# Bias broadcasts of the first layer issued from GpSimd behind marker copies, and two more weight-chunk buffers from the first layer on

## The chip, the core and the metric

The kernel runs on one core of one Trainium2 chip. The time is device microseconds (us) of that core. In the text PE is TensorE, DVE is VectorE, ACT is ScalarE, POOL is GpSimd and SP is SyncE. Each of these engines works through its own list of instructions in order. A transfer (DMA) is started by an instruction in the list of SP, ACT or POOL, and all transfers then run on the same 16 DMA engines.

## What is computed

The program is a whole small network on 512 tokens of width 1024: a first block of two layers and a second block with a state-space mixer and a convolutional feed-forward. The change touches only the first layer of the first block and a table that later attention stages use:

```python
def short_conv_mixer(h, w_in, conv_w, w_out):
    b_gate, c_gate, u = jnp.split(h @ w_in, 3, axis=-1)
    v = c_gate * u
    vp = jnp.pad(v, ((0, 0), (CONV_WIDTH - 1, 0), (0, 0)))
    conv = sum(conv_w[k] * vp[:, k:k + S] for k in range(CONV_WIDTH))
    return (b_gate * conv) @ w_out

def squared_relu_mlp(h, w1, w2):
    return jnp.square(jax.nn.relu(h @ w1)) @ w2
...
        bias_w = jnp.transpose(bias_g[t5_bucket(d_w)], (0, 2, 3, 1))   # d_w: query position minus key position
        logit_w = jnp.einsum('bqghd,bkgd->bqghk', qt, kw) + bias_w[None]
```

The attention bias depends only on the distance of query and key, so for each head it is one line of numbers, shifted by one element from one query to the next.

## The kernel before, in words

**Weights.** All weight matrices lie in DRAM as 362 chunks of 128x1024 f32 (512 KB), in the order in which PE will take them. `Stream.pre` (L188) loads a chunk ahead into a buffer `w32` (two buffers) with a DMA issued by SP (L195), and splits it by halves of 128x512 into a high part `whi` (ACT, L214) and a low part `wlo` (DVE, L216), four buffers each. Three matmuls of 128x128 by 128x512 (high by high, high by low, low by high) use each 128x128 block, so a chunk is 8 x 3 = 24 matmuls. PE takes `whi` and `wlo`; the buffers of a half come free when PE has finished with the half four before it, and a `w32` buffer comes free when both its halves are split. While the field `ap` of the stream is set, that is in the two MLP stages (chunks 34 to 95 and 135 to 196), two chunks of every four go into two further buffers `ax`, so that four chunks are held.

**First layer.** `layer_a` (L516) makes eight blocks f = 0 to 7 of the gated convolution. A block is three products of 24 matmuls each (c, u and b gate, one chunk apiece), then a short run on DVE and ACT: `cc`, `v`, three convolution steps `cv`, `b`, the block's output `o` (L561), and its split `yh` (ACT, L320) and `yl` (DVE, L321). Five tiles per block come from a ring of ten. The products lie in seven PSUM buffers. Then eight products with `a_w_out` follow, and the MLP.

**Bias lines.** In block f = 1 `biases` (L609) computes the 16 lines of numbers with six small matmuls and stores them to DRAM as `line` (SP, L625; the scheduler puts its parts between other work, so that it ends in block 3). `skew_out` (L635) then broadcasts a stretch of a head's line to 128 rows of a DRAM table `sk`, each row one element longer than the stretch, so that a later plain read sees every row shifted by one. There are 48 such DRAM-to-DRAM transfers: 16 of 128x640 (320 KB), 16 of 128x384 (192 KB) and 16 of 128x144 (72 KB). `skew_out` is called after each product from block 2 on, two transfers a call, and they are issued by ACT (L638). The tables are first read at 629 us, in the attention stage.

**Order.** A scheduler orders each engine's list when the program is built. `keep_in_program_order` keeps the transfers in the order of the code among themselves. Each DMA signals its landing on one of eight semaphores that are handed out in turn, and a DMA that gets a semaphore still in use waits for the transfer that has it. Those issued by SP and ACT share one set of eight (`DMAHW0` to `DMAHW7` in the rows below), those issued by POOL have another (`DMASW0` to `DMASW7`).

Of the kernel before, what the change touches and what calls it, by code (L numbers as in the profile page):

```python
# [10 lines left out]
F32 = mybir.dt.float32  # L11
# [8 lines left out]
P = 128  # L20
# [25 lines left out]
PPB = 9  # L46
NSA_CH = (96, 133)
MIX_CH = (197, 272)
MLP_CH = ((34, 96), (135, 197))
AHEAD = (7, 8)  # L50


# [74 lines left out]
class Stream:  # L127
    def __init__(self, b, pool, src, nch):
        self.b, self.pool, self.src, self.nch = b, pool, src, nch
        self.order = []  # L130
        self.w32, self.hl = {}, {}
        self.nd = self.ns = 0
        self.pos = 0
        self.lo_mod = 0
        self.plan = {}
        self.dlo = None
        self.ap = None
        self.todo = list(range(*NSA_CH)) + list(range(*MIX_CH))
        self.done = set()
        self.owed = 0  # L140

    def aux(self, c):
        return self.ap is not None and any(a <= c < b for a, b in MLP_CH)

    def scaled(self, half):
        g, ks = self.plan[half]
# [41 lines left out]
    def pre(self, half):  # L188
        b, nc = self.b, self.b.nc
        while self.nd < min(self.nch, half // 2 + (4 if self.aux(half // 2 + 3) else 2)):  # L190
            if self.aux(self.nd) and self.nd % 4 < 2:
                t = self.ap.tile([P, 1024], F32, tag="ax", name="ax", bufs=2)
            else:
                t = self.pool.tile([P, 1024], F32, tag="w32", name="w32", bufs=2)
            nc.sync.dma_start(t, self.src[self.nd])  # L195
            self.w32[self.nd] = t
            self.nd += 1
        while self.ns < min(2 * self.nch, half + 3):
            c, o = divmod(self.ns, 2)
            src = self.w32[c][:, o * 512:o * 512 + 512]  # L200
            h = self.pool.tile([P, 512], F32R, tag="whi", name="whi", bufs=4)
            l = self.pool.tile([P, 512], F32R, tag="wlo", name="wlo", bufs=4)
            if c in self.done:
                nc.sync.dma_start(l.bitcast(F32), self.dlo[c][:, o * 512:o * 512 + 512])
                parts = self.scaled(self.ns) if self.ns in self.plan else [(slice(0, 512), 1.0)]
                for a, sc in parts:
                    nc.scalar.activation(out=h[:, a], in_=src[:, a], func=AF.Copy, scale=sc)  # L207
            elif self.ns in self.plan:
                for a, sc in self.scaled(self.ns):
                    nc.scalar.activation(out=h[:, a], in_=src[:, a], func=AF.Copy, scale=sc)  # L210
                    nc.vector.scalar_tensor_tensor(out=l[:, a], in0=src[:, a], scalar=sc, in1=h[:, a].bitcast(F32),
                                                   op0=ALU.mult, op1=ALU.subtract)
            else:
                nc.scalar.activation(out=h, in_=src, func=AF.Copy)  # L214
                eng = nc.gpsimd if self.ns % 4 < self.lo_mod else nc.vector
                eng.tensor_tensor(out=l, in0=src, in1=h.bitcast(F32), op=ALU.subtract)  # L216
            self.hl[self.ns] = (h, l)
            if o:
                del self.w32[c]
            self.ns += 1  # L220
# [18 lines left out]
class Builder:  # L239
# [230 lines left out]
    def first(self):  # L470
        nc, tc = self.nc, self.tc
        self.xs = [self.X() for _ in range(KD)]
        self.load0()
        st = self.st
        ld = lambda k: nc.sync.dma_start(self.xs[k][:, 16:528], self.a["x"][:, k * 512:k * 512 + 512])
        st.begin((0, 512))
        ld(0)
        ld(1)
        st.begin((512, 1024))
        ld(2)  # L480
        ld(3)
        st.begin((0, 1024))
        for k in range(4, KD):
            ld(k)
        self.loads()
        with ExitStack() as c:
            ps = c.enter_context(tc.tile_pool(name="psA", bufs=1, space=PSUM))
            self.ps1 = lambda: ps.tile([P, 512], F32, tag="mm", bufs=7, name="mm")
            self.pst = lambda: ps.tile([P, 512], F32, tag="st", bufs=1, name="st")
            with ExitStack() as c2:  # L490
                self.yp = c2.enter_context(tc.tile_pool(name="la", bufs=1))
                self.layer_a()
            if self.stop == "a":
                return
            self.st.ap = c.enter_context(tc.tile_pool(name="ahead", bufs=1))
            self.mlp("mlp_w1_0", "mlp_w2_0", "g_mlp0")
            self.st.ap = None
        if self.stop == "mlp0":
            return
        self.st.lo_mod = LO1  # L500
        with ExitStack() as c:
            self.nsa(c)
        self.st.lo_mod = 0
        if self.stop == "nsa":
            return
        with ExitStack() as c:
            ps = c.enter_context(tc.tile_pool(name="psC", bufs=1, space=PSUM))
            self.ps1 = lambda: ps.tile([P, 512], F32, tag="mm", bufs=7, name="mm")
            self.pst = lambda: ps.tile([P, 512], F32, tag="st", bufs=1, name="st")
            self.st.ap = c.enter_context(tc.tile_pool(name="ahead", bufs=1))  # L510
            self.mlp("mlp_w1_1", "mlp_w2_1", "g_mlp1")
            self.st.ap = None

    def layer_a(self):
        nc = self.nc
# [13 lines left out]
        for f in range(KD):  # L529
            pcs = []  # L530
            for part in (1, 2, 0):
                if f == 0 and part:
                    p = (p1, p2)[part - 1]
                else:
                    p = self.ps1()
                    self.gemm([(p, XS)], "a_w_in", 0, part * 1024 + f * 128, hs)
                    self.skew_out()
                pcs.append(p)
                if f == 0 and part == 0:
                    d = self.stat1(acc, 1024, self.pst, (0, 0))  # L540
                    r = self.stat2(d, self.pst, (0, 0))
                    r2 = self.base.tile([P, W], F32, tag="rstd", bufs=2, name="r2")
                    nc.vector.tensor_tensor(out=r2[:, XS], in0=r[:, XS], in1=r[:, XS], op=ALU.mult)
            if f == 1:
                self.biases()
            pc, pu, pb = pcs
            cc = tt("cc")
            nc.vector.tensor_tensor(out=cc, in0=pc, in1=r2[:, XS], op=ALU.mult)
            v = tt("v")
            nc.vector.tensor_tensor(out=v, in0=pu, in1=cc, op=ALU.mult)  # L550
            w = lambda k: self.pv("acw", k * 8 + f)
            t = tt("cv")
            nc.scalar.activation(out=t, in_=v, func=AF.Copy, scale=w(2))
            nc.vector.scalar_tensor_tensor(out=t[:, 1:512], in0=v[:, 0:511], scalar=w(1), in1=t[:, 1:512],
                                           op0=ALU.mult, op1=ALU.add)
            nc.vector.scalar_tensor_tensor(out=t[:, 2:512], in0=v[:, 0:510], scalar=w(0), in1=t[:, 2:512],
                                           op0=ALU.mult, op1=ALU.add)
            b = tt("b")
            nc.vector.tensor_tensor(out=b, in0=pb, in1=r[:, XS], op=ALU.mult)
            o = tt("o")  # L560
            nc.vector.tensor_tensor(out=o, in0=b, in1=t, op=ALU.mult)  # L561
            yh, yl = yt("yh"), yt("yl")
            self.split(yh, yl, o)
            ys.append((yh, yl))
        for m in range(KD):
            p = self.ps1()
            self.gemm([(p, slice(0, 512))], "a_w_out", 0, m * 128, ys)
            self.skew_out()
            x = self.xs[m]
            nc.vector.tensor_tensor(out=x[:, XS], in0=p, in1=x[:, XS], op=ALU.add)  # L570

# [57 lines left out]
        self.skews = [(h, sk, a, n) for sk, a, n in ((self.sk1, 0, 640), (self.sk2, OH_A, 384), (self.sk3, OH_A + 384, 144))  # L629
                      for h in range(16)]  # L630

    skews = ()

    def skew_out(self):
        for _ in range(min(2, len(self.skews))):  # L635
            h, sk, a, n = self.skews.pop(0)
            self.tc.keep_in_program_order(
                self.nc.scalar.dma_start(sk[h:h + 1, :].rearrange("o (q w) -> (o q) w", w=n + 1)[:, 0:n],  # L638
                                         self.line[h:h + 1, a:a + n].to_broadcast([128, n])))

    def skew(self, sk, h, n):
        return sk[h:h + 1, 0:128 * n].rearrange("o (q w) -> (o q) w", w=n)
# [1254 lines left out]
```

## Time and profile before

| | |
|---|---|
| three runs | 2440.92, 2446.57, 2449.51 us; median 2446.57 |
| the profiled execution's own time | 2439.07 us |
| its span, first to last instruction | 2437.3 us |
| PE busy | 2360.5 us, 97% of the span |
| DVE, ACT, POOL busy | 1643.9, 1234.4, 450.0 us |
| mean granted TensorE clock | 0.991 of 2.4 GHz |

The span leaves 1.8 us of the execution's time outside it. Times in the text count from the span's start. PE is nearly always busy, so what matters is where it is not, and where its clock is below 1.

### The profile page before, as it was taken

To read this page: it belongs to the slowest core of one execution; us is meant where nothing else is said; L and a number is where in the kernel's file an instruction comes from. 1 tells how busy PE (TensorE), PEld (TensorE's weight loads), DVE (VectorE), ACT (ScalarE), POOL (GpSimd) and SP (SyncE) were. 2 spreads that over 40 slices of the span, in tenths; PEclk is the share of its full clock that TensorE was granted. 3 is DMA by queue.
4 is the path that set the end of the run, shared out by engine and by line. 5 is a ranking of instruction groups with operands and counts; after the bars stand their busy time and mean duration, and the time that the engine had idled before them with its cause. 6 is when DMAs were issued, how large, how long until landed. Compare 5 with 4: busy or idle time off the path is not lost.

```text
span 2437.3 us, 38984 instructions
## 1 busy us (share of the span) xinstructions
PE 2360.5 (97%) x14369; PEld 2067.7 (85%) x14369; DVE 1643.9 (67%) x3260; ACT 1234.4 (51%) x2431; POOL 450.0 (18%) x609
## 2 busy tenths in 40 slices
PE   8899999999999999999999999999999999999997
PEld 6688888887787777888889999999989999998996
DVE  6356856765767768657757895578875566864873
ACT  4135544444777765434555776556564334432442
POOL 1001111122223322111242222023331100000001
PEclk9999999999999999999999999999999999999998
DMA  4576777787643446777776445645456362322322
GB/s 147 149 160 201 271 253 266 249 280 219 225 134 96 134 131 242 264 264 250 267 243 197 128 147 177 187 152 161 145 156 190 104 197 87 94 89 96 93 90 78
DMA packets 160491, 427.39 MB, mean 175 GB/s; under 512 B 23131, under 2 KB 33627, under 8 KB 160251
## 3 DMA queue, kind: packets, MB, share of 16 engines
q1 hardware_dynamic: 119680, 296.15, 38.1%
q0 software_dynamic: 32576, 117.92, 14.4%
q10 hardware_dynamic: 8044, 10.83, 2.4%
q8 instruction: 113, 1.85, 0.3%
q14 instruction: 78, 0.64, 0.1%
HBM read 349.01 MB, written 83.29 MB: 177 GB/s over the span
## 4 chain that ended last, share of the span: by engine, by line
PE 80%; DVE 7%; DMA 5%; ACT 4%; issue 2%; ACTq 0%; POOL 0%; SPq 0%; POOLq 0%; DVEq 0%
PE mm L312 69%; PE g L312 3%; PE o L312 3%; DMA L<-csd 3%; PE s L312 2%; PE pt L316 1%; DMA w<-in_ws_dram 1%; ACT L L1564 1%; PE u L316 1%; DVE e L744 1%; DVE pl L321 1%; DVE cvt L1351 1%; DVE Ml L321 1%; PE u L312 1%; ACT ph L320 1%
## 5 line engine op out<-in xcount | busy, mean ns | idle before, releaser
L312 PE MATMUL mm<-hh,whi 128*128 128x258 f32 (+2 forms) x2464 | 796.9, 324 | 26.4 <-ACT whi L214 12.4
L312 PE MATMUL mm<-hl,whi 128*128 128x258 f32 (+2 forms) x2464 | 795.7, 323 | 2.7 <-DVE hl L361 2.6
L312 PE MATMUL mm<-hh,wlo 128*128 128x258 f32 (+2 forms) x2464 | 797.8, 324 | 0.2 <-DVE ms L427 0.2
L312 PEld LDWEIGHTS mm<-hh,whi 128*128 128x128 f32 x2464 | 464.3, 189 | 70.2 <-ACT whi L214 14.1
L312 PEld LDWEIGHTS mm<-hl,whi 128*128 128x128 f32 x2464 | 464.7, 189 | 44.0 <-DVE hl L361 4.2
L312 PEld LDWEIGHTS mm<-hh,wlo 128*128 128x128 f32 x2464 | 464.9, 189 | 40.2 <-issue 2.4
L214 ACT ACTIVATE whi<-w 128x512 fp32r<-128x512 f32 x378 | 237.8, 631 | 487.6 <-PE mm L312 362.4
L216 DVE TENSOR_TENSOR wlo<-w,whi 128x512 fp32r<-128x512 f32 x376 | 263.8, 703 | 218.2 <-ACT whi L214 209.3
L312 PE MATMUL mm<-b,whi 128*128 128x512 f32 (+1 forms) x699 | 273.5, 391 | 0.0
L312 PE MATMUL mm<-a,wlo 128*128 128x512 f32 (+1 forms) x699 | 273.5, 391 | 0.0
L312 PE MATMUL mm<-a,whi 128*128 128x512 f32 (+1 forms) x699 | 273.0, 391 | 0.0
L178 POOL DMA_DIRECT2D dlo<-al x112 | 60.5, 540 | 545.1 <-DVE al L177 427.1
L312 PEld LDWEIGHTS mm<-a,wlo 128*128 128x128 f32 x699 | 131.7, 188 | 29.8
L312 PEld LDWEIGHTS mm<-b,whi 128*128 128x128 f32 x699 | 131.7, 188 | 29.8
L312 PEld LDWEIGHTS mm<-a,whi 128*128 128x128 f32 x699 | 131.7, 188 | 29.7
L214 ACT ACTIVATE whi<-ax 128x512 fp32r<-128x512 f32 x122 | 76.9, 631 | 146.6 <-PE mm L312 146.5
L207 ACT ACTIVATE whi<-w 128x512 fp32r<-128x512 f32 x182 | 111.8, 623 | 62.4 <-PE mm L312 55.6
L177 DVE TENSOR_TENSOR al<-aw,ah 128x1024 fp32r<-128x1024 f32 x91 | 115.9, 1274 | 24.7 <-ACT ah L176 24.7
L216 DVE TENSOR_TENSOR wlo<-ax,whi 128x512 fp32r<-128x512 f32 x122 | 83.8, 688 | 70.2 <-ACT whi L214 70.0
L312 PE MATMUL mm<-oh,whi 128*128 128x258 f32 (+1 forms) x400 | 123.1, 309 | 2.4 <-ACT oh L320 2.1
L312 PE MATMUL mm<-ol,whi 128*128 128x258 f32 (+1 forms) x400 | 122.0, 305 | 0.3 <-DVE ol L321 0.3
L312 PE MATMUL mm<-oh,wlo 128*128 128x258 f32 (+1 forms) x400 | 121.8, 305 | 0.0
(538 smaller groups left out, 4424.1 us busy)
## 6 DMA issues: line engine op xcount, KB each, us to landing
w<-in_ws_dram SPq DMA_DIRECT2D x300, 512.0 KB, 4.2
aw<-in_ws_dram POOLq DMA_DIRECT2D x112, 512.0 KB, 6.1
dlo<-al POOLq DMA_DIRECT2D x112, 512.0 KB, 3.0
wlo<-dlo SPq DMA_DIRECT2D x224, 256.0 KB, 3.1
ax<-in_ws_dram SPq DMA_DIRECT2D x61, 512.0 KB, 5.8
L<-csd SPq DMA_DIRECT2D x32, 256.0 KB, 3.8
sk<-line ACTq DMA_DIRECT2D x16, 320.0 KB, 12.0
bias<-sk SPq DMA_DIRECT2D x16, 256.0 KB, 3.7
```

The source lines that it names most:

```text
L177: nc.vector.tensor_tensor(out=l, in0=w, in1=h.bitcast(F32), op=ALU.subtract)
L178: nc.gpsimd.dma_start(self.dlo[c], l.bitcast(F32))
L207: nc.scalar.activation(out=h[:, a], in_=src[:, a], func=AF.Copy, scale=sc)
L214: nc.scalar.activation(out=h, in_=src, func=AF.Copy)
L216: eng.tensor_tensor(out=l, in0=src, in1=h.bitcast(F32), op=ALU.subtract)
L312: self.nc.tensor.matmul(out, l, r, start=start, stop=stop)
L316: self.nc.tensor.transpose(out, in_, self.ident[0:n, 0:n])
L320: nc.scalar.activation(out=hi, in_=src, func=AF.Copy)
L321: (eng or nc.vector).tensor_tensor(out=lo, in0=src, in1=hi.bitcast(F32), op=ALU.subtract)
L744: (nc.gpsimd if g in EPOOL else nc.vector).tensor_tensor(out=ev[64 * q:64 * q + 64, :, g, 0:nn], in0=src[:, q, 4 * jh:4 * jh + 4, b:b + nn ...
L1351: nc.vector.scalar_tensor_tensor(out=t[:, s:W], in0=u[:, 0:W - s], scalar=hw(k), in1=t[:, s:W], op0=ALU.mult, op1=ALU.add)
L1564: nc.scalar.activation(out=L[:, cx * 128:cx * 128 + 128], in_=L[:, cx * 128:cx * 128 + 128], func=AF.Relu, scale=-1.0, bias=self.cs[:, cx ...
```

## The change

The 48 broadcasts are issued by POOL instead of ACT. They are no longer called after each product; in each block f = 1 to 7, `skew_out(o, 7)` first copies one column of the block's output `o` to a small tile (`mark`, a POOL copy of 128x1) and then issues up to seven broadcasts on POOL. The two `ax` buffers get a pool of their own that is open from the first layer on, and the chunks that may use them start with chunk 4 instead of 34.

```diff
-MLP_CH = ((34, 96), (135, 197))
+DEEP_CH = ((4, 96), (135, 197))
...
-        return self.ap is not None and any(a <= c < b for a, b in MLP_CH)
+        return self.axp is not None and any(a <= c < b for a, b in DEEP_CH)
...
             if self.aux(self.nd) and self.nd % 4 < 2:
-                t = self.ap.tile([P, 1024], F32, tag="ax", name="ax", bufs=2)
+                t = self.axp.tile([P, 1024], F32, tag="ax", name="ax", bufs=2)
...
             self.pst = lambda: ps.tile([P, 512], F32, tag="st", bufs=1, name="st")
+            self.st.axp = c.enter_context(tc.tile_pool(name="ax", bufs=1))
...
                     self.gemm([(p, XS)], "a_w_in", 0, part * 1024 + f * 128, hs)
-                    self.skew_out()
...
             yh, yl = yt("yh"), yt("yl")
+            if f:
+                self.skew_out(o, 7)
             self.split(yh, yl, o)
...
             self.gemm([(p, slice(0, 512))], "a_w_out", 0, m * 128, ys)
-            self.skew_out()
...
-    def skew_out(self):
-        for _ in range(min(2, len(self.skews))):
-            h, sk, a, n = self.skews.pop(0)
-            self.tc.keep_in_program_order(
-                self.nc.scalar.dma_start(sk[h:h + 1, :].rearrange("o (q w) -> (o q) w", w=n + 1)[:, 0:n],
-                                         self.line[h:h + 1, a:a + n].to_broadcast([128, n])))
+    def skew_out(self, after, n):
+        nc, pin = self.nc, self.tc.keep_in_program_order
+        mark = self.sm("mark")
+        nc.gpsimd.tensor_copy(mark[:, 0:1], after[:, 0:1])
+        for _ in range(min(n, len(self.skews))):
+            h, sk, a, w = self.skews.pop(0)
+            pin(nc.gpsimd.dma_start(sk[h:h + 1, :].rearrange("o (q w) -> (o q) w", w=w + 1)[:, 0:w],
+                                    self.line[h:h + 1, a:a + w].to_broadcast([128, w])))
```

The lists of the engines show what this moves. First ACT, around the splits of chunk 13 (`w_767` before, `ax` after). Before:

```order
L214 ACTIVATE whi<-w_767 128x512
L638 DMA sk_493<-line 128x640 x12
L320 ACTIVATE yh<-o 128x512
L214 ACTIVATE whi<-w_767 128x512
L638 DMA sk_493<-line 128x640 x2
L214 ACTIVATE whi<-w_804 128x512 x2
L638 DMA sk_493<-line 128x640 x2
L553 ACTIVATE cv<-v,pkt 128x512
```

and with the change, from the first half of chunk 12 on:

```order
L214 ACTIVATE whi<-ax 128x512 x2
L554 ACTIVATE cv<-v,pkt 128x512
L214 ACTIVATE whi<-ax 128x512 x2
L320 ACTIVATE yh<-o 128x512
L214 ACTIVATE whi<-w_729 128x512 x2
L214 ACTIVATE whi<-w_789 128x512 x2
L554 ACTIVATE cv<-v,pkt 128x512
```

ACT's list no longer has any broadcast between the two halves of a chunk. Next POOL, whose list had nothing here between the sums of the first and of the second normalisation; it now reads (with what each row waits for, as far as it is a semaphore):

```order
L637 COPY mark<-o 128x1 [waits DVE_49] x2
L640 DMA sk_500<-line 128x640 [waits DMAHW0_49]
L640 DMA sk_500<-line 128x640 x7
L640 DMA sk_500<-line 128x640 [waits DMASW0_49]
L640 DMA sk_500<-line 128x640 [waits DMASW1_49]
L640 DMA sk_500<-line 128x640 [waits DMASW2_49]
L640 DMA sk_500<-line 128x640 [waits DMASW3_49]
L640 DMA sk_500<-line 128x640 [waits DMASW4_49]
L640 DMA sk_500<-line 128x640 [waits DMASW5_49]
L637 COPY mark<-o 128x1 [waits DVE_49]
L640 DMA sk_500<-line 128x640 [waits DMASW6_49]
L640 DMA sk_500<-line 128x640 [waits DMASW7_49]
```

The markers of blocks 1 and 2 stand together, fourteen broadcasts follow them, and the marker of block 3 comes behind these; from the ninth broadcast on each waits for the one eight before it. Last SP, around the store of `line`: before (chunks 14, 15, 16 and 17)

```order
L195 DMA w_804<-in_ws_dram 128x1024 [waits DMAHW3_49,DVE_49]
L625 DMA line<-la 16x2256 [waits DVE_49]
L195 DMA w_841<-in_ws_dram 128x1024 [waits DMAHW6_49,DMAHW4_49,DVE_49]
L195 DMA w_894<-in_ws_dram 128x1024 [waits DMAHW5_49,DMAHW0_49,DVE_49]
L195 DMA w_931<-in_ws_dram 128x1024 [waits DMAHW6_49,DMAHW4_49,DVE_49]
```

and with the change (chunks 16, 17, 18, 19 and 20)

```order
L195 DMA ax<-in_ws_dram 128x1024 [waits DMAHW3_49,DVE_49]
L627 DMA line<-la 16x2256 [waits DVE_49]
L195 DMA ax<-in_ws_dram 128x1024 [waits DMAHW4_49,DVE_49]
L195 DMA w_919<-in_ws_dram 128x1024 [waits DMAHW5_49,DVE_49]
L195 DMA w_954<-in_ws_dram 128x1024 [waits DMAHW6_49,DVE_49]
L195 DMA ax<-in_ws_dram 128x1024 [waits DMAHW7_49,DVE_49]
```

Two chunks more are asked for ahead of `line`, and the semaphores that the chunk loads wait for no longer pass through a broadcast. Past the start of the first MLP the lists of all engines are the same in both programs, but for names and line numbers.

## Rows read from the trace of the kernel before

**Rows 1.** Waits of PE from 0 to 230 us: who waited for whom, us in total, times, longest.

```profile
PE mm L312 <- ACT whi L214: 11.8, 2, 8.6
PE mm L312 <- ACT hh L360: 6.8, 1, 6.8
PE mm L312 <- DVE hl L361: 2.6, 2, 2.4
```

**Rows 2.** Busy time by stretch. Columns: stretch and its length, busy us (x instructions) of PE, of weight loads, of DVE, ACT, POOL, then granted clock, busy share of the DMA engines, GB/s.

```profile
84.00:94.00 10.00, 9.95 (x44) 7.74 (x42) 2.14 (x4) 0.00 (x0) 0.00 (x0) 1.00 0.64 125
94.00:102.50 8.50, 0.00 (x0) 0.00 (x1) 0.54 (x1) 1.15 (x2) 0.00 (x0) 0.79 0.86 206
102.50:112.40 9.90, 9.90 (x36) 7.70 (x36) 4.24 (x7) 1.87 (x3) 0.00 (x0) 0.83 0.94 225
112.40:116.00 3.60, 0.39 (x2) 0.20 (x2) 0.22 (x1) 0.88 (x2) 0.00 (x0) 1.00 0.61 242
116.00:120.00 4.00, 4.00 (x11) 2.94 (x11) 4.00 (x7) 2.06 (x4) 0.00 (x0) 0.57 0.69 125
120.00:200.00 80.00, 80.00 (x346) 64.72 (x346) 41.26 (x60) 28.42 (x45) 5.19 (x4) 1.00 0.68 155
```

**Rows 3.** PE in order of time around its two gaps: start, duration, engine, line, operation; in brackets the idle time before and what ended it.

```profile
93.55 0.40 PE L312 MATMUL mm<-hh,wlo 128*128 128x512 f32 x1
102.50 0.79 PE L312 MATMUL mm<-hh,whi 128*128 128x512 f32 x1 [8.55 <-ACT whi L214]
103.09 0.63 PE L312 MATMUL mm<-hl,whi 128*128 128x512 f32 x1
...
105.96 0.39 PE L312 MATMUL mm<-hh,wlo 128*128 128x512 f32 x1
...
112.19 0.40 PE L312 MATMUL mm<-hh,wlo 128*128 128x512 f32 x1
115.80 0.61 PE L312 MATMUL mm<-hh,whi 128*128 128x512 f32 x1 [3.21 <-ACT whi L214]
...
119.59 0.40 PE L312 MATMUL mm<-hh,whi 128*128 128x512 f32 x1
```

**Rows 4.** ACT in order of time in the same stretch; ACTq is a DMA issue in ACT's list, with the time from its first to its last.

```profile
82.71 0.63 ACT L214 ACTIVATE whi<-w 128x512 fp32r<-128x512 f32 x1 [1.95 <-PE mm L312]
84.73 16.52 ACTq L638 DMA_DIRECT2D sk<-line  x12
101.30 0.63 ACT L320 ACTIVATE yh<-o 128x512 fp32r<-128x512 f32 x1 [17.96 <-DMA sk<-line]
101.41 1.75 ACTq L638 DMA_DIRECT2D sk<-line  x1
101.83 0.61 ACT L214 ACTIVATE whi<-w 128x512 fp32r<-128x512 f32 x1
...
115.12 0.63 ACT L214 ACTIVATE whi<-w 128x512 fp32r<-128x512 f32 x1 [6.59 <-DMA w<-in_ws_dram]
```

**Rows 5.** DVE in the same stretch: the output of block 3.

```profile
86.39 0.69 DVE L561 TENSOR_TENSOR o<-b,cv 128x512 f32<-128x512 f32 x1
```

**Rows 6.** The chain of waits from 76 to 125 us: start, duration, what.

```profile
81.01 3.70 DMA line<-la
...
92.13 12.09 DMA sk<-line
104.22 0.02 issue
104.24 0.03 SPq L195
104.27 0.03 issue
104.30 10.72 DMA w<-in_ws_dram
```

**Rows 7.** Waits of SP's list from 76 to 120 us.

```profile
SPq L195 <- DMA sk<-line: 34.1, 3, 22.8
SPq L195 <- DVE wlo L216: 8.7, 3, 6.0
```

**Rows 8.** DMA queues from 84 to 104 us (packets, MB, share of 16 engines; q10 is ACT's), and the issues in it: count, KB each, median us to landing.

```profile
q10 hardware_dynamic: 1412, 3.24, 73.5%
...
sk<-line ACTq DMA_DIRECT2D x14, 320.0 KB, 11.8
```

**Rows 9.** All chunk loads L195 from 60 to 200 us: time to landing.

```profile
DMA to landing us min/median/max: 3.5/5.3/10.7
```

**Rows 10.** Busy time, columns as in rows 2: the first MLP, where four chunk buffers are in use already and POOL issues transfers (`aw`, `dlo`), and the part of it in which DVE is busiest.

```profile
240.00:560.00 320.00, 320.00 (x1382) 259.51 (x1381) 220.72 (x334) 158.35 (x264) 59.96 (x106) 1.00 0.77 265
...
240.00:260.00 20.00, 20.00 (x88) 16.26 (x87) 19.97 (x38) 13.14 (x26) 3.17 (x6) 1.00 0.81 272
```

**Rows 11.** DMA queues of POOL (q0) and SP (q1) from 240 to 560 us, and issues in it, columns as in rows 8.

```profile
q0 software_dynamic: 14716, 53.55, 49.7%
q1 hardware_dynamic: 8928, 30.94, 27.1%
...
aw<-in_ws_dram POOLq DMA_DIRECT2D x50, 512.0 KB, 6.1
w<-in_ws_dram SPq DMA_DIRECT2D x30, 512.0 KB, 5.7
```

**Rows 12.** POOL in order of time, the first work of the program, a sum of 128x512, and its first two transfers.

```profile
0.24 0.10 POOL L1879 MEMSET const-float32-0.0<- 128x1 f32 x1 [0.24 <-issue]
...
180.86 1.29 POOL L346 TENSOR_TENSOR acc<-sq 128x512 f32<-128x512 f32 x1 [164.29 <-ACT sq L341]
...
212.72 1.30 POOL L165 DMA_DIRECT2D aw<-in_ws_dram  x2 [8.61 <-PE mm L312]
```

**Rows 13.** All issues of line L165 on POOL: ns min/median/max, first and last start.

```profile
L165 POOL DMA_DIRECT2D aw<-in_ws_dram x112: 527/527/747, 212.7 to 1265.5; - x112
```

More of the change, by code (lines that the diff above doesn't have):

```diff
@@ L136, in __init__ @@
         self.dlo = None
-        self.ap = None
+        self.ap = self.axp = None
         self.todo = list(range(*NSA_CH)) + list(range(*MIX_CH))
@@ L496, in first @@
             self.mlp("mlp_w1_0", "mlp_w2_0", "g_mlp0")
-            self.st.ap = None
+            self.st.ap = self.st.axp = None
         if self.stop == "mlp0":
@@ L509, in first @@
             self.pst = lambda: ps.tile([P, 512], F32, tag="st", bufs=1, name="st")
+            self.st.axp = c.enter_context(tc.tile_pool(name="ax", bufs=1))
             self.st.ap = c.enter_context(tc.tile_pool(name="ahead", bufs=1))
             self.mlp("mlp_w1_1", "mlp_w2_1", "g_mlp1")
-            self.st.ap = None
+            self.st.ap = self.st.axp = None
     def layer_a(self):
@@ L630, in biases @@
                       for h in range(16)]
-    skews = ()
-    def skew_out(self):
-        for _ in range(min(2, len(self.skews))):
-            h, sk, a, n = self.skews.pop(0)
-            self.tc.keep_in_program_order(
-                self.nc.scalar.dma_start(sk[h:h + 1, :].rearrange("o (q w) -> (o q) w", w=n + 1)[:, 0:n],
-                                         self.line[h:h + 1, a:a + n].to_broadcast([128, n])))
+    def skew_out(self, after, n):
[6 more added lines that the diff above has]
+                                    self.line[h:h + 1, a:a + w].to_broadcast([128, w])))
     def skew(self, sk, h, n):
```

## Prediction, made before the changed kernel ran

> **What bounds the kernel now.** PE is busy 97% of the span, so I looked only for where it is not, in four steps. The waits of PE up to 230 us give 21.2 us of idle time [rows 1]. The two waits for `hh` and `hl` belong to the first 18 us of the program, before any broadcast, and stay. The rest is 11.8 us behind the split `whi` of a weight chunk, in two pieces. The table by stretch shows where: PE does nothing from 94 to 102.5 us and next to nothing from 112.4 to 116, and behind each gap the granted clock falls (0.83 over ten microseconds, 0.57 over four) [rows 2]. The rows of PE in order of time give both gaps their edges [rows 3]. ACT's rows and the chain of waits tell who is late [rows 4, 6].
>
> The reader should see two different causes. **First gap:** `line` lands at 84.7 us, and ACT, which has just split the first half of chunk 13, meets twelve broadcasts in its list. They hold it from 84.73 to 101.25, and the split of the second half, which PE needs at 93.8, starts at 101.83. The block's output `o` was ready at 87.1 [rows 5], its split `yh` waited for ACT until 101.30. **Second gap:** SP's loads waited 34.1 us for broadcasts, once 22.8 us [rows 7], because both queues draw from one set of semaphores. So the load of chunk 15 went out only at 104.30 and, beside the broadcasts, took 10.72 us to land [rows 6], twice the median of 5.3 [rows 9]. ACT's split at 115.12 ends that gap.
>
> **What the two gaps cost.** Undisturbed, PE makes 346 matmuls in 80 us, 0.231 us each [rows 2], hence 24 x 0.231 = 5.55 us a chunk. Gap one: from 93.55 + 0.23 to 102.50, 8.72 us. Gap two: from 112.19 + 0.23 to 115.80, 3.38 us. From 102.50 to 105.96 PE makes 8 matmuls at the lower clock, 1.2 instead of 2.4 GHz (36 lie in the stretch to 112.4, and 28 of them fill it from 105.96 on), in 3.46 us instead of 1.85: 1.61 lost. From 115.80 to 119.59 it makes 9 (the 11 of the row from 116 to 120, less the last two), in 3.79 instead of 2.08: 1.71 lost. **Together 8.72 + 3.38 + 1.61 + 1.71 = 15.4 us.** Between 120 and 200 us PE runs on at 0.231 although six broadcasts a block still go out, so there is nothing more to win there, nor before 84 us.
>
> **The change, part by part.** *Broadcasts off ACT.* 48 issues leave ACT's list. What counts is the twelve between the halves of chunk 13: without them `whi` can follow as soon as PE frees its buffer, at about 85.5 us, 8 us before PE wants it. Gap one and its slow spell go: 8.72 + 1.61 = 10.3 us. ACT's other issues held nobody that PE waits for: I cost them at nothing.
>
> *Broadcasts on POOL.* POOL does nothing from 84 to 120 us and 5 us of work from there to 200 [rows 2]. A transfer costs POOL 0.53 us, 0.75 at most [rows 13], so 48 are 25 to 36 us of an idle engine. The marker, a copy of 128x1, has no row; it lies between a memset of that size, 0.10 us, and a sum of 128x512, 1.29 us [rows 12]; I take 0.1, and at the upper end seven are 9 us of idle POOL, so the path sees zero at either end. What queues behind a waiting marker is only further broadcasts, whose tables are first read at 629 us, and the sums of the next normalisation at 180 us; block 7, whose marker is the last, ends near 87.1 + 4 x 16.65 = 154.
>
> *Pace.* The markers of blocks 1 and 2 are passed before `line` exists, and the one of block 3 at 87.1 us. So they hold back nothing at first: 21 broadcasts are free to go at about 85 us, not seven. What holds them is the eight semaphores of POOL: no more than eight are under way. A 320 KB broadcast takes 73.5% of 20 us for 3.24 MB, that is 4.54 us a MB and 1.49 us of all engines [rows 8]; one of 192 KB 0.89 us. The 21 are 16 x 1.49 + 5 x 0.89 = 28.3 us of DMA time, eight in flight 11.9 us.
>
> *Four chunks instead of two, and own semaphores.* When the burst starts, chunks 13 to 15 are there and 16 is on its way, since SP asks for 16 ahead of `line`. Chunk 17 goes out near 86 us, before most of the burst. Chunk 18 is the first that meets it: it takes the buffer of 14, whose second half is split when PE leaves chunk 12 at 91.0, so it goes out at about 92.5. PE reaches it at 96.55 + 4 x 5.55 = 118.75 and wants it landed at 117.3, with the two splits ahead of it. It has 24.8 us. How long a load takes beside broadcasts from POOL no row shows. The lower bound is 5.7 us, the median of `w` in the MLP, where POOL's transfers fill half of all DMA time and four buffers kept PE without a gap for 320 us [rows 10, 11]. The upper is 10.7 us, the worst beside ACT's broadcasts [rows 6, 9]. I take 10.7, the nearer in kind; either fits twice. Gap two goes with its slow spell: 3.38 + 1.71 = 5.1 us.
>
> Two more loads of 512 KB start near 11 us. They stand behind `x` in SP's own queue, so they cost the start nothing; if that cover were gone, two loads of 1.5 us each (27.1% of 320 us for 30.94 MB is 2.80 us a MB [rows 11]) would be the price. Beyond the first layer both programs have the same lists.
>
> **Sum.** 10.3 + 5.1 = 15.4 us less, 0.63%. The profiled execution's own time is 2439.07 us (span 2437.3): 2423.7 after. That execution is 7.5 us below the median 2446.57, whose like is 2431.2. The mean of the four times shown is 2444.0; I take it as base: 2444.0 - 15.4 = **2429 us**.
>
> **One rule against it.** The rows say that moving the broadcasts frees ACT and parts the semaphores. The Trainium skill, DMA: Bandwidth & Descriptors, section Issuing engines are not separate DMA queues, says that transfers started from different engines run on the same 16 DMA engines and that another issuer saves only the issuing time. By that rule the bytes and the slow landing stay as they were; that is the second case below, and the sum by it would be 10.3 us.
>
> **The rivals.**
>
> *Only gap one goes.* The 48 broadcasts still take 16 x (1.49 + 0.89 + 0.33) = 43 us of all DMA engines, so a chunk may come late as before. For it: 94% busy from 102.5 to 112.4 [rows 2], and a load that took 10.7 us. Against it: chunk 18 has 24.8 us, and at 10.7 us a load two under way at a time keep step with 5.55 us a chunk. Price: gap two and its spell stay, 2444.0 - 10.3 = 2434 us. Chance 0.10.
>
> *The burst only moves (the markers do not do what they say).* Loads wait out the whole burst of 21, and broadcasts from POOL take 1.3 times as long: 84.7 + 1.3 x 28.3 + two loads of 1.5 + a landing of 3.5 + two splits of 1.4 = 129.4, so PE stands 10.7 us before chunk 18, and 1.7 us go to the lower clock. That leaves 3 us: 2441 us, no difference that can be told (a measurement of this kernel tells some 0.3%, 7 us). Against it: eight in flight, 11.9 us, is the most that a load can find ahead of it, and POOL's queue takes 2.97 us a MB in the MLP against 2.80 for SP's [rows 11], not 1.3 times. Chance 0.09.
>
> *The markers hold the first layer (slower).* Marker 3 reads `o` of block 3 and stands behind fourteen broadcasts in POOL's list. The ring of ten tiles gives that buffer again to `o` of block 5, at 87.1 + 2 x 3 x 5.55 = 120.4 us. If the marker has not run by then DVE stops, and with four more PSUM buffers PE stops 22 us later, at 143. To end slower than before the marker must come 15.4 us later still, at 158: POOL would have to be held 5.2 us by each broadcast. Were it held for the whole landing, 11.8 us [rows 8], marker 3 would run at 250 and the time be 2444.0 - 15.4 + 107 = 2536 us. Against it: POOL's first two transfers take it 1.30 us together [rows 12], though such a load needs 6.1 us to land [rows 11]; with eight in flight the fourteenth goes out when the sixth has landed, near 100 us. The Trainium skill, SBUF — State Buffer, section SBUF: two separate sides, warns that certain VectorE operations lock GpSimd out while it writes a transfer's descriptors, and gives 3.1 us instead of 0.62 as an example. By that figure, an estimate, marker 3 would come at 128 us, late for DVE and still before PE stops. The trace speaks against much of it: with DVE busy 19.97 of 20 us [rows 10], no issue took over 0.75 us [rows 13]. Chance 0.03.
>
> **How the numbers follow.** Forecast 0.78, the others 0.10, 0.09 and 0.03. Forecast and first rival are faster by over 0.3%: 0.88. The second rival is the same: 0.09. Slower: 0.03. The range takes the forecast from 2423.7 (the profiled base) to 2431 (the median base), 2.5 us below for scatter of the runs, and the first rival up to 2446.57 - 10.3 = 2436: 2421 to 2437. The outer two cases lie outside.
>
> **What would show it.** In the profile after: no gap of PE between 20 and 230 us and a granted clock of 1.00 in every stretch there; ACT's `yh` of block 3 near 87 us; no wait of SP for a broadcast; 14 broadcasts on POOL from 85 us on and marker 3 near 100 us; chunk loads landing within 11 us. A gap that ends in `whi` near 117 to 135 us, behind a chunk load, would say that the cover was too short; a DVE row that waits for POOL would say that the markers hold; a gap anywhere later would break the claim that nothing else moves.

## The result and the profile after

The changed kernel takes 2426.89 us, median of four runs (2426.18 to 2430.19), against 2444.51 before (four runs, 2440.92 to 2449.51). The ratio is 0.9929 with a 95% interval of 0.9913 to 0.9945, which is 13 to 21 us less. The forecast was 2429 with a range of 2421 to 2437. That range also holds the first rival's 2434, so the time alone does not part the two; the waits and the mark below do. The profiled execution of the changed kernel takes 2430.19 us, with a span of 2428.4.

First the waits of PE from 0 to 230 us in the changed kernel, columns as in [rows 1]:

```profile
PE mm L312 <- ACT hh L360: 6.7, 1, 6.7
PE mm L312 <- DVE hl L361: 2.4, 1, 2.4
```

The 11.8 us behind `whi` are gone; what is left belongs to the first 18 us. The busy time by stretch, in the stretches of [rows 2] and one ahead of them:

```profile
18.00:22.00 4.00, 4.00 (x12) 3.09 (x12) 4.00 (x12) 0.58 (x2) 0.00 (x0) 0.57 0.56 147
...
84.00:94.00 10.00, 10.00 (x45) 8.14 (x44) 5.23 (x8) 3.16 (x5) 4.89 (x10) 1.00 0.68 151
94.00:102.50 8.50, 8.50 (x39) 6.90 (x38) 4.17 (x6) 2.62 (x4) 2.09 (x4) 1.00 0.93 258
102.50:112.40 9.90, 9.90 (x45) 8.04 (x44) 4.54 (x7) 3.04 (x5) 2.84 (x5) 1.00 0.99 286
112.40:116.00 3.60, 3.60 (x17) 2.94 (x16) 1.85 (x3) 1.18 (x3) 1.05 (x2) 1.00 1.01 249
```

PE is full and its granted clock is 1.00 through all four stretches in which [rows 2] show the gaps and the lower clock. The DMA engines are busier there than before (from 94 to 116 us 0.93 to 1.01 of their time, against 0.61 to 0.94), so the broadcasts have not gone away; they only hold nobody. The first row is the exception: from 18 to 22 us the granted clock is 0.57 (the lower level for most of it), and PE makes 12 matmuls. The same stretch of the kernel before reads

```profile
18.00:22.00 4.00, 4.00 (x18) 3.26 (x19) 4.00 (x11) 0.91 (x2) 0.00 (x0) 1.00 0.61 147
```

18 matmuls, six more, which are 6 x 0.231 = 1.4 us. ACT in order of time in the changed kernel, against [rows 4]:

```profile
84.15 0.63 ACT L214 ACTIVATE whi<-ax 128x512 fp32r<-128x512 f32 x1 [1.95 <-PE mm L312]
86.94 0.63 ACT L214 ACTIVATE whi<-ax 128x512 fp32r<-128x512 f32 x1 [2.15 <-PE mm L312]
89.03 0.63 ACT L320 ACTIVATE yh<-o 128x512 fp32r<-128x512 f32 x1 [1.47 <-DVE o L562]
```

The second half of chunk 13 is split at 86.94, not at 101.83; `yh` follows `o` at once. POOL, which now has the broadcasts (second column: time from the first to the last of the group):

```profile
53.85 0.19 POOL L637 COPY mark<-o 128x1 f32<-128x1 f32 x1 [37.33 <-DVE o L562]
69.80 0.19 POOL L637 COPY mark<-o 128x1 f32<-128x1 f32 x1 [15.77 <-DVE o L562]
86.42 4.37 POOL L640 DMA_DIRECT2D sk<-line  x8 [16.43 <-DMA line<-la]
91.69 0.53 POOL L640 DMA_DIRECT2D sk<-line  x1 [0.91 <-DMA sk<-line]
...
103.80 0.52 POOL L640 DMA_DIRECT2D sk<-line  x1 [2.13 <-DMA sk<-line]
104.32 0.75 POOL L637 COPY mark<-o 128x1 f32<-128x1 f32 x1
```

Eight go out in one row, and from the ninth on each waits for an earlier one. Marker 3 runs at 104.32, behind the fourteenth. SP's list from 76 to 120 us, against [rows 7]:

```profile
SPq L195 <- DVE wlo L216: 43.2, 8, 6.1
```

It waits only for buffers, no longer for a broadcast. The DMA queues from 84 to 104 us, against [rows 8] (q0 is POOL's, q1 SP's):

```profile
q0 software_dynamic: 592, 2.48, 57.9%
q1 hardware_dynamic: 441, 1.64, 23.8%
...
sk<-line POOLq DMA_DIRECT2D x14, 320.0 KB, 16.6
w<-in_ws_dram SPq DMA_DIRECT2D x2, 512.0 KB, 11.4
ax<-in_ws_dram SPq DMA_DIRECT2D x1, 512.0 KB, 12.3
```

The chunk loads in this stretch land late, after 11.4 and 12.3 us, and nobody feels it. Last the chain of waits. Before and after have the same two `st` matmuls in the first MLP, past the last broadcast; before:

```profile
115.80 103.56 PE mm L312 x438
219.36 0.86 PE st L312 x2
```

and after:

```profile
81.56 123.82 PE mm L312 x533
205.38 0.86 PE st L312 x2
```

The chain no longer leaves PE. The mark comes 219.36 - 205.38 = 14.0 us earlier: the 15.4 us of the forecast less the 1.4 us lost at 18 to 22 us. This mark is the sharpest measure of the change, since only 205 us of a run lie ahead of it. Of the 14.0 us, the spans of these two executions keep 2437.3 - 2428.4 = 8.9. The other 5 us went later, where both programs have the same lists. Matched matmul by matmul (times of the kernel before), the lead is 14.0 us at the mark, 15.9 at 1260 us, 17.8 at most (at 1494 us) and 9.9 at the last matmul. One piece of the loss, 3.1 us, falls into this stretch:

```profile
1550.00:1600.00 50.00, 49.37 (x380) 47.52 (x379) 35.46 (x63) 26.68 (x52) 9.24 (x7) 0.93 0.49 154
```

The granted clock is 0.93 in it and 1.00 in the same stretch of the kernel before. The other three runs of the change have spans 3.2 to 4.0 us shorter than the profiled one, so I read this as the scatter of executions.

### The profile page after: what moved, and what is told of

Same layout as the page of the kernel before. It is cut to its first block, busy times and chain, and to the rows that moved or that the text cites. A ratio compares the mean times of both kernels' runs of the same rounds, so it can differ in the third digit from the quotient of the medians.

```text
span 2428.4 us, 38996 instructions
## 1 busy us (share of the span) xinstructions
PE 2360.5 (97%) x14369; PEld 2070.6 (85%) x14369; DVE 1644.6 (68%) x3260; ACT 1235.7 (51%) x2431; POOL 475.9 (20%) x664
## 4 chain that ended last, share of the span: by engine, by line
PE 83%; DVE 8%; ACT 4%; DMA 3%; issue 2%; SPq 0%; DVEq 0%; ACTq 0%
PE mm L312 72%; PE g L312 3%; PE o L312 3%; DMA L<-csd 2%; PE s L312 2%; PE pt L316 1%; PE u L316 1%; DVE e L746 1%; ACT L L1566 1%; DVE cvt L1353 1%; PE u L312 1%; DVE pl L321 1%; DVE Ml L321 1%; ACT ph L320 1%; DMA w<-in_ws_dram 0%
## 5 line engine op out<-in xcount | busy, mean ns | idle before, releaser
L312 PE MATMUL mm<-hh,whi 128*128 128x258 f32 (+2 forms) x2464 | 796.1, 324 | 14.6 <-ACT hh L360 6.7
L214 ACT ACTIVATE whi<-w 128x512 fp32r<-128x512 f32 x346 | 218.3, 631 | 435.5 <-PE mm L312 334.9
L216 DVE TENSOR_TENSOR wlo<-w,whi 128x512 fp32r<-128x512 f32 x344 | 242.3, 705 | 191.7 <-ACT whi L214 184.6
L214 ACT ACTIVATE whi<-ax 128x512 fp32r<-128x512 f32 x154 | 97.3, 632 | 211.1 <-PE mm L312 206.2
L216 DVE TENSOR_TENSOR wlo<-ax,whi 128x512 fp32r<-128x512 f32 x154 | 105.9, 687 | 85.8 <-ACT whi L214 85.5
L207 ACT ACTIVATE whi<-w 128x512 fp32r<-128x512 f32 x182 | 111.8, 623 | 66.0 <-PE mm L312 59.8
```

The lines of the kernel that those rows point to most:

```text
L312: self.nc.tensor.matmul(out, l, r, start=start, stop=stop)
```

## The experiments

Two theories stood. **Mine:** gap one was twelve issues between two halves in ACT's list (10.3 us), gap two a chunk load that waited for the broadcasts' semaphores (5.1 us); POOL, its pace and the markers cost nothing, and the extra buffers little by themselves. **The rivals:** the extra buffers carry a good part, because loads beside broadcasts are too slow for two buffers; or the broadcasts as such (their bytes, their place in POOL's list) are near a limit.

**Broadcasts on POOL, but two buffers in the first layer.**

```diff
-DEEP_CH = ((4, 96), (135, 197))
+DEEP_CH = ((34, 96), (135, 197))
```

> The change without its deeper buffers: broadcasts from POOL behind markers, but two chunk buffers in the first layer. My theory: what cost 15.4 us was ACT held by twelve broadcasts and SP's loads held by semaphores that broadcasts used; both are gone. With two buffers chunk 15 goes out near 88 us and PE reaches it near 102, so a load has about 13 us, and beside POOL's broadcasts it took 12.3 at most: gaps of PE behind whi of 2 us at most in sum between 84 and 140 us, time 2427 to 2430, no wait of SP for a broadcast. Rival (the buffers cure the second gap): a gap of 3 us or more behind a chunk load with a slow spell of 1.7, time about 2432.

Measured: 2433.72 us (six runs, 2431.68 to 2438.6), ratio 0.9960 (0.9948 to 0.9972). Its chain of waits:

```profile
102.48 11.88 DMA w<-in_ws_dram
...
117.05 8.88 DMA w<-in_ws_dram
...
128.62 10.94 DMA w<-in_ws_dram
...
139.67 0.64 ACT whi L214
...
209.84 0.86 PE st L312 x2
```

The chain has left PE for the chunk loads: each goes out when a chunk's second half is split, lands 9 to 12 us later and is split at once. The mark comes 4.5 us later than with four buffers, 0.5 of which was lost ahead of 82 us. There is no large gap; PE waits for `whi` twice, 1.5 us in all, and the rest is thinly spread:

```profile
114.00:124.00 10.00, 9.80 (x40) 6.89 (x39) 4.29 (x7) 3.03 (x5) 3.35 (x7) 1.00 0.99 273
134.00:144.00 10.00, 8.75 (x37) 6.49 (x37) 4.27 (x7) 1.88 (x3) 1.69 (x4) 1.00 0.99 193
```

37 and 40 matmuls where undisturbed PE makes 43. So my expectation, 2427 to 2430, missed, and the first rival is right here: with POOL as the issuer the extra buffers are worth 4 us at the mark, more than I gave them.

**Four buffers, but the broadcasts on ACT, two after each product, as before.** The edit is the change's part on the `ax` pool and `DEEP_CH` alone, on the kernel before:

```diff
-MLP_CH = ((34, 96), (135, 197))
+DEEP_CH = ((4, 96), (135, 197))
...
+            self.st.axp = c.enter_context(tc.tile_pool(name="ax", bufs=1))
```

> The change without its POOL part: four chunk buffers, broadcasts issued by ACT two after each product as before. My theory: ACT still meets twelve broadcasts between the halves of chunk 13, so the first gap stays (8 to 9 us plus 1.6 at the lower clock); the second goes, because chunks 14 to 16 are there when ACT is free again: 2444.5 - 5.1 = 2439. Rival (slow landing beside the broadcasts is the cause, deeper buffers the cure): no gap, 2427 to 2430. Second rival (SP's semaphore waits hold even four buffers): both gaps stay, 2444.

Measured: 2436.35 us (twelve runs, 2428.9 to 2444.98), ratio 0.9966 (0.9953 to 0.9980). Its waits of PE behind `whi`:

```profile
PE mm L312 <- ACT whi L214: 8.0, 1, 8.0
```

and of SP's list from 60 to 200 us behind broadcasts:

```profile
SPq L195 <- DMA sk<-line: 40.9, 7, 23.3
```

Gap one is nearly as before (8.0 us against 8.6), gap two is gone, and its `st` mark stands at 215.28, which is 4.1 us ahead of before and 9.9 behind the change. SP still waits for broadcasts, once 23.3 us, as long as before, but with four chunks held that wait is covered. So the second gap can be taken away alone, and both are of the sizes that the sum gave them (10.3, and 5.1 less the early low-clock spell, which this execution has too).

**The change without markers.**

```diff
-        mark = self.sm("mark")
-        nc.gpsimd.tensor_copy(mark[:, 0:1], after[:, 0:1])
```

> The change without the marker copies: all 48 broadcasts stand together in POOL's list and are free to go when the line has landed. My theory: the markers hold next to nothing, since 21 were free at once already and eight under way is the real limit; a load lands within 13 us and has 24: no gap of PE, the same time as the change, 2425 to 2430. Rival (the markers' pace protects the loads): broadcasts fill the DMA engines without a break to about 150 us, loads fall behind, gaps of 3 to 10 us after 117 us, 2430 to 2437.

Measured: 2428.75 us (six runs, 2424.35 to 2432.84), ratio 0.9933 (0.9920 to 0.9945); no wait of PE behind `whi`, the `st` mark at 205.32. POOL's waits from 0 to 160 us:

```profile
POOL sk L638 <- DMA line<-la: 69.7, 1, 69.7
POOL sk L638 <- DMA sk<-line: 41.0, 32, 3.9
```

The eight semaphores alone pace the broadcasts. At this load the markers neither help nor harm.

**Each broadcast twice on POOL**, the second into a table that nobody reads; this doubles the traffic and the list, with the markers in place.

```diff
+            tw = self.twin[w]
+            pin(nc.gpsimd.dma_start(tw[h:h + 1, :].rearrange("o (q w) -> (o q) w", w=w + 1)[:, 0:w],
+                                    self.line[h:h + 1, a:a + w].to_broadcast([128, w])))
```

> The change with each broadcast issued twice, the second time into a table that nobody reads: 96 transfers, twice the load on the DMA engines. My theory: at most eight are under way, a load has 24 us and lands within about 13 however long the burst, so PE has no gap up to 160 us; the sums of the next normalisation on POOL come later, behind the last broadcasts (near 195 instead of 167 us), and cost 0 to 3 us: 2427 to 2430. Rival (the traffic itself is the cost and the change only just covers it): loads get less than the 95 GB/s that PE eats, the four buffers run dry after 120 us, gaps of 10 us or more, 2437 or more.

Measured: 2478.06 us (four runs, 2471.9 to 2482.73), ratio 1.0138 (1.0120 to 1.0155), slower than before. PE's two gaps with what ended them:

```profile
178.79 0.79 PE L312 MATMUL mm<-yh,whi 128*128 128x512 f32 x1 [17.49 <-ACT yh L320]
248.60 0.80 PE L312 MATMUL mm<-hh,whi 128*128 128x512 f32 x1 [25.81 <-ACT whi L214]
```

PE stands from 161 and from 223 us. One step back, on DVE and on ACT:

```profile
177.38 0.69 DVE L562 TENSOR_TENSOR o<-b,cv 128x512 f32<-128x512 f32 x1 [22.23 <-POOL mark L638]
```

```profile
247.40 0.63 ACT L341 ACTIVATE sq<-x 128x512 f32<-128x512 f32 x1 [33.58 <-POOL acc L346]
```

The first gap is the mechanism of the third rival of the prediction, at twice the load: `o` finds its buffer held by a marker that is late in POOL's list. The second: the sums `acc` of the next normalisation stand behind the last broadcasts (POOL reaches the first at 246.10), ACT's `sq` waits for them, and the splits wait behind `sq`. Between 84 and 144 us, with the DMA engines 0.92 busy, PE had no gap. So the traffic did not starve the loads there; the order of POOL's list did the harm. I had priced these sums at 0 to 3 us, so the expectation of 2427 to 2430 missed, and I ran one more kernel.

**Twice, without markers, and the sums of that normalisation on DVE.**

```diff
-                (nc.vector if k >= 6 else nc.gpsimd).tensor_tensor(
+                (nc.gpsimd if late and k < 6 else nc.vector).tensor_tensor(
...
-        mark = self.sm("mark")
-        nc.gpsimd.tensor_copy(mark[:, 0:1], after[:, 0:1])
```

> Each broadcast twice as in the run before (96 transfers), but without marker copies, and with the sums of the later normalisations on VectorE instead of GpSimd, so that nothing else that PE needs stands in POOL's list behind the broadcasts. My theory now: the 33 us that doubling cost came from POOL's order (VectorE waited 27 us for markers, the sums stood behind broadcasts to 246 us) and none from the traffic; a load lands within 19 us and has 24: no gap of PE behind whi from 84 to 230 us, 2426 to 2432. Rival (the traffic starves the loads): gaps behind whi of 10 us or more after 120 us, 2440 or more.

Measured: 2474.07 us (four runs, 2472.09 to 2478.67), ratio 1.0122 (1.0108 to 1.0135). By time the expectation, 2426 to 2432, missed. The stretches tell why:

```profile
144.00:164.00 20.00, 20.00 (x88) 16.16 (x87) 10.31 (x16) 7.40 (x12) 3.66 (x7) 1.00 0.98 233
164.00:184.00 20.00, 20.00 (x87) 16.09 (x86) 12.87 (x20) 9.41 (x15) 6.27 (x12) 1.00 0.97 207
184.00:204.00 20.00, 20.00 (x87) 16.14 (x86) 10.25 (x16) 7.53 (x12) 6.27 (x12) 1.00 0.97 231
204.00:224.00 20.00, 7.74 (x32) 5.63 (x30) 0.00 (x0) 0.00 (x0) 9.28 (x18) 0.78 0.90 127
224.00:244.00 20.00, 0.00 (x0) 0.00 (x0) 0.00 (x0) 0.00 (x0) 9.86 (x20) 0.50 0.91 72
```

PE runs without a gap from 84 to 211.7 us, with the DMA engines 0.97 to 0.98 busy in the three full stretches, though chunk loads take 12.4 us in the median. This execution has no early spell, and up to its stop it shows what the two gaps are worth by themselves. The mark in PE's own order of time, in the kernel before and here (the chain of waits counts it some 0.16 us later):

```profile
219.20 1.02 PE L312 MATMUL st<-acc,ones 128*128 128x512 f32 x2
203.79 1.02 PE L312 MATMUL st<-acc,ones 128*128 128x512 f32 x2
```

That is 15.4 us, the sum of the forecast. Then PE stands for 44.7 us. ACT's row at the end of that:

```profile
253.38 2.44 ACT L172 ACTIVATE ah<-aw,pkt 128x128 fp32r<-128x128 f32 x8 [53.11 <-DMA aw<-in_ws_dram]
```

POOL's first load `aw` (L165, the first of [rows 12, 13]) stood behind all 96 broadcasts and went out at 245.90; ACT, whose list has `ah` next, waited 53.1 us for it, and the splits of PE's weights stood behind `ah`. I had overlooked it. Doubled traffic alone did not starve PE in 120 us; what stopped it was a third instruction that the list delayed.

**The kernel before, with the broadcasts on ACT spread otherwise:** none ahead of block 4, then three after each product instead of two; ACT issues, two buffers.

```diff
-                    self.skew_out()
+                    if f > 3:
+                        self.skew_out()
...
-        for _ in range(min(2, len(self.skews))):
+        for _ in range(min(3, len(self.skews))):
```

> The kernel before with the broadcasts left on ACT and two chunk buffers, but called only from block 4 on, three after each product, so that no twelve of them pile up behind the line. My theory: what made the first gap was the pile of twelve between the halves of one chunk, not ACT as the issuer; with at most three between two splits ACT is held for 1 to 5 us and the first gap goes. The loads still share their semaphores with broadcasts and have two buffers, so some 4 to 6 us of small gaps behind whi stay, as with POOL and two buffers: 2431 to 2436. Rival (any broadcast in ACT's list holds the splits for its turn): gaps of 8 us or more in sum, 2438 to 2445.

Measured: 2425.88 us (five runs, 2424.53 to 2429.06), ratio 0.9924 (0.9912 to 0.9937), below the 2431 to 2436 that I expected. The 4 to 6 us of small gaps did not come: PE has no wait behind `whi` up to 260 us, and the `st` mark stands at 204.94, which is 14.4 us ahead of before, without an early spell. ACT's waits for loads show how near it is; one of its rows:

```profile
129.77 0.63 ACT L214 ACTIVATE whi<-w 128x512 fp32r<-128x512 f32 x1 [4.52 <-DMA w<-in_ws_dram]
```

This split is on the chain, yet PE is busy 9.87 of the ten microseconds around it. SP never waits for a broadcast here, though it still shares its semaphores with them. The pile in ACT's list was the cause of both gaps; neither POOL nor the buffers are needed to take it away.

**The change again**, beside the last two on their chip, without an edit.

> The change itself once more, beside the other two on the same chip: 2425 to 2431, no gap of PE between 20 and 230 us. No rival; it is the measure for the other runs and for the scatter of one profiled execution.

Measured: 2430.41 us (five runs, 2426.8 to 2434.38), ratio 0.9938 (0.9924 to 0.9951); no wait behind `whi`, the `st` mark at 205.51. The spread on ACT has the lower median, by 4.5 us, but the intervals overlap and five runs of each do not settle which is faster. At the mark the change pays 1.4 to 1.6 us for the early spell and the spread 1.0 for its loads. Nothing I ran clearly beats the change.

## Why the prediction was right, step by step

- **Gap one, 10.3 us: right.** The split moved from 101.83 to 86.94, within 1.4 us of the 85.5 that I gave, and 1.4 us is what the early spell had cost by then. The kernel that keeps ACT's twelve is 9.9 us later than the change at the mark.
- **Gap two, 5.1 us: right in size, but its cause was in the main misread.** I put its cover to "four chunks instead of two, and own semaphores" and did not divide it. More buffers alone remove the gap (broadcasts on ACT, four buffers). The semaphores held the load of chunk 15 much less than I said. With two buffers it takes the buffer of chunk 13, and that was not free before the split that gap one had delayed was done, in the kernel before at 102.57 + 0.69 = 103.26:

```profile
102.57 0.69 DVE L216 TENSOR_TENSOR wlo<-w,whi 128x512 fp32r<-128x512 f32 x1
```

The broadcast that SP waited for landed at 104.22 [rows 6], so it cost this load 1.0 us and not 22.8: the row of waits [rows 7] puts a wait for several things down to the one that came last. So the gaps do not have two different causes, as I had written; the second followed from the first, with a load of 10.72 us and only two buffers behind it. The spread on ACT agrees: two buffers, shared semaphores, and neither gap. Own semaphores alone do not quite do it: with two buffers on POOL, loads of 9 to 12 us cost 4 us, in many small pieces and not as one gap. So with broadcasts from POOL four chunks are needed.

- **Cover for chunk 18: right by a wide margin.** The slowest load from 60 to 200 us took 12.3 us, more than the 10.7 that I took as the upper bound and the 11 that I named as the sign; the cover that I had worked out was 24.8. Why the bound was too low is not shown: the slowest load left with four broadcasts under way, and the one that gave the bound with five.
- **Pace: right in kind, early in size.** 14 broadcasts go out from 86.4 on and marker 3 at 104.3, said "near 100". Everything stands 1.4 us later by the early spell; the rest is the landing, 16.6 us in the median and not 11.8.
- **Markers and POOL, zero: right.** A marker takes 0.18 to 0.75 us (I took 0.1), and the kernel without them gives the same time. The 48 issues took 0.52 to 0.73 us each. The warning of the Trainium skill, SBUF — State Buffer, section SBUF: two separate sides, did not show here: DVE was busy 44 of the 80 us from 120 to 200, and no issue was held. What DVE ran there was TENSOR_TENSOR and SCALAR_TENSOR_TENSOR alone, so the case says nothing of its other operations.
- **A clock of 1.00 everywhere from 20 to 230: wrong** in one place, 18 to 22 us, 1.4 us. I had counted nothing ahead of 84 us. Such a spell is in both profiles of the change and in those of every experiment built on it but one (the last with doubled broadcasts), and not in those of before and of the spread on ACT. Two loads more start near 11 us in these kernels, but the kernel with two buffers has the spell without them and the exception has them without the spell. What goes with it in all nine profiles is when PE first reaches the upper level of its clock. In the three without the spell its matmuls follow each other at 0.23 us from 10.4 us on at the latest; in the six with it they still come at 0.43 us, the lower level, and go over only between 10.8 and 12.7 us. The same matmul before and after:

```profile
10.54 0.39 PE L312 MATMUL mm<-hh,wlo 128*128 128x512 f32 x1
10.74 0.63 PE L312 MATMUL mm<-hh,wlo 128*128 128x512 f32 x1
```

Behind this PE stands for 2.4 us in both kernels (`hl`, up to 17.8 us), and the clock falls only in the one that rose later. Whether the change or chance delays the rise is not shown, so the cause stays open.

- **The rule against the change.** POOL's broadcasts took 57.9% of 20 us for 2.48 MB, 4.67 us a MB, against 4.54 from ACT, and they landed late as before. The Trainium skill, DMA: Bandwidth & Descriptors, section Issuing engines are not separate DMA queues, says that transfers run on the same 16 DMA engines whichever engine started them; the trace agrees. The same section of the Trainium skill says that another issuer saves only the issuing time, which is usually small beside the transfer. For one broadcast that holds (0.56 to 2.80 us an issue, 11.8 to landing), but twelve in a row held ACT's list for 16.52 us [rows 4], and PE stood for the split behind them. The spread on ACT shows that this was a matter of order in the list and not of the engine.
- **The rivals.** "Only gap one goes" and "the burst only moves" fell with the waits of PE. "The markers hold the first layer" is a real mechanism that decides at some point between this load and twice this load.

The medians differ by 17.6 us where 15.4 were forecast and 14.0 show at the mark; the interval, 13 to 21, holds all three. The mark bears the forecast out; that the median also came within 2.1 us of it is partly luck, since the lead of one execution over another wanders by some 8 us behind the mark. From 22 us to the mark PE now has no gap and its clock is 1.00, so there is nothing more to win there.

## What to carry to other kernels

Before moving transfers to another engine, read what stands in line behind them on the engine that they leave and on the one that they join: the gain came from freeing the splits behind twelve issues, and the doubled versions lost it all through a marker, a sum and a load that stood behind the broadcasts on POOL. A few issues between two pieces of critical work, rather than all of them as soon as their data is there, can do as much as another engine and more buffers. Where a slow transfer can't be helped, count how many microseconds of work the buffers ahead hold, and compare it with the slowest landing beside that traffic, not with the median.

## What the runs showed of the hardware that was not expected

- A 320 KB broadcast within DRAM landed 16.6 us after its issue from POOL and 11.8 from ACT, at the same cost of DMA time per MB. POOL had eight of them under way in this stretch; ACT, which shares its eight semaphores with SP's loads, had five to seven from 90 us on. Eight beside chunk loads would give the longer time: 8 x 0.328 MB x 4.67 = 12.2 us of all engines, and with 57.9 of 82% busy for the broadcasts 12.2 x 82 / 57.9 = 17.3 us (an estimate).
- With the DMA engines 0.97 to 0.98 busy for 60 us (doubled broadcasts, no markers) chunk loads still landed within 14.6 us and PE lost nothing.
- A POOL copy of 128x1 took 0.18 to 0.20 us six times and 0.75 once, at 104.32 behind a broadcast; two others right behind a broadcast took 0.20.
- The early spell at the lower clock level described above: it goes with a clock that first rose 0.4 to 2 us later, and its cause is open.
